# A diffusion block of pooling mixer, RG-LRU and ConvFFN: the sums of w_down, the second modulation rows and half of a modulation change their places

## The chip, the cores and the metric

The kernel runs on one core of a Trainium2 chip. The metric is device time in microseconds from launch to end. Engines are named as in the profile: PE is TensorE, DVE VectorE, ACT ScalarE, POOL GpSimd, SP SyncE. Each engine works through one queue in order; transfers are issued from SP's queue and from POOL's.

## The reference

One layer over 1024 latent tokens of width 1024 (a 16 x 64 grid) with 256 context tokens, float32.

```python
sh1, sc1, ga1, sh2, sc2, ga2 = split(silu(c) @ w_mod + b_mod, 6)
hx = rmsnorm(x, g_pre_mix) * (1 + sc1) + sh1            # hc likewise, from ctx and c_ctx
u_pool, u_lru, u_gate, g_pool, g_lru = split(h @ w_in)
y_pool = pooled windows of u_pool, less u_pool, @ pool_w, * pool_scale
y_lru  = (h_f + h_b) * gelu(u_gate)                     # two scans over conv(u_lru), context first
m = sigmoid(g_pool) * (y_pool @ w_proj_pool) + sigmoid(g_lru) * (y_lru @ w_proj_lru)
x = x + ga1 * rmsnorm(m @ w_out, g_post_mix)
g, u = split((rmsnorm(x, g_pre_ffn) * (1 + sc2) + sh2) @ w_up)
f = (gelu(conv3x3(g) + b) * u) @ w_down
x = x + ga2 * rmsnorm(f, g_post_ffn)
```

## The kernel before

All products run as three fp32r matmuls: each operand is split into a high and a low part (`split`: a cast on ScalarE, then a subtraction on VectorE), and hi*hi, hi*lo and lo*hi are summed. Weights come in tiles of 128 x 1024 (512 KB) through three SBUF buffers of the tag "raw" and are split into three buffers of the tag "whl" (`load_w`); so a load waits on SP's queue until a raw buffer is free, and a cast waits until a unit has left its whl buffer. Rows of w_mod, the short rows of `rowv`, x and w_up use the same three raw buffers.

The framework fixes the order of each engine's queue when the program is built, by the order of the program, moved by `high_priority` and `issue_after`; a tile is given out when an earlier one of its tag is released, which is after its last reader.

The stages, in order:
- **Start.** The first two parts of the modulation (`mod_block`), norm and transpose of x in two token halves, and `modulate`: high part on ScalarE, the product in float32 on GpSimd, low part on VectorE, for eight columns of 128 channels a half.
- **Input projections.** Units of 48 matmuls from hx for the pooled branch (`pool_unit`, `pool_out`), the u gates (`ug_unit`) and some g gates; results go to DRAM (yp_d, gl_d, sg_d) through GpSimd's queue. `mod_steps` walks over w_mod for the rows 0 and 1 of the later modulation (gate 1 and shift 2): eight loads of 512 KB, each multiplied into `acc` on VectorE; then `ones`-matmuls ("pm") add over the partitions, and one or two short rows, loaded into raw buffers, are added or multiplied to it, and the result is stored to row_d. `some(mods, 3)` makes three of the nine steps of a row.
- **LRU.** For each of eight channels of 128: `lru_in` (projection and convolution), `lru_scan` (gates, the square of r on GpSimd, two scans, times gl, store to yl_d), and a g gate. Rows 2 and 3 (scale 2, gate 2) of `mod_steps` go in between, three steps a channel.
- **Projections.** yp and yl are loaded by GpSimd's queue and split, six more g gates, then `pp_unit` (y_pool @ w_proj_pool) and `pl_unit` (y_lru @ w_proj_lru): pp 0 to 3, then pl 0, pp 4, pl 1, pp 5, pl 2, pp 6, pl 3, pp 7, pl 4 to 7. After pl 2, 3 and 4 `form_pair` loads two w_up tiles (ru, rg) and stores sums of them for the FFN. After pl 4 and 5 four tiles of w_out each are loaded. The results go to m_d.
- **Out projection**, x1, norm, second modulation and transposes for eight token tiles (L691 to L729).
- **FFN.** 24 blocks f of 128 channels; products in the form of Strassen and Winograd, seven half products of 12 matmuls a block (`mid`, `tail`, `head`), weights formed on VectorE (`weights`), a 3 x 3 convolution on VectorE (`post`), gu stored by GpSimd's queue. Beside it the queue sums quarters of w_down with accumulating DMAs in `n2raw` and stores them to sd_d (`sum_steps`): five steps for each of twelve p, three steps a block in the blocks 0 to 19.
- **Down projection**, again seven products, from w_down, sd_d and gu_d; `finish` normalises a token tile, adds x1 and stores it.

Of the kernel before, what the change touches and what calls it, by code (L numbers as in the profile page):

```python
# [14 lines left out]
D = 1024  # L15
# [25 lines left out]
def block_kernel(ctx: ExitStack, tc: tile.TileContext, x, cx, vecs, rowv, icnt, w_mod1, w_mod, w_in, pool_w,  # L41
# [58 lines left out]
    n2raw = gpool.tile([P, 4, 512], F32, name="n2raw", tag="n2raw")  # L100
    epsc = cpool.tile([P, 1], F32, name="epsc")
# [45 lines left out]
    def modulate(dst_hi, dst_lo, src, k, which):  # L147
        A.activation(dst_hi, src, AF.Identity, scale=S1[:, k, which:which + 1], bias=B1[:, k, which:which + 1])
        G.tensor_scalar(src, src, S1[:, k, which:which + 1], B1[:, k, which:which + 1],
                        op0=ALU.mult, op1=ALU.add)  # L150
        V.tensor_sub(dst_lo, src, f32(dst_hi))
# [10 lines left out]
    with tc.tile_pool(name="z0", bufs=1, reuse_waits="tile") as zp:  # L162
# [36 lines left out]
        def mod_x(h, k):  # L199
            modulate(hx[:, h, k, 0, :], hx[:, h, k, 1, :], xT[h][:, k, :], k, 0)  # L200
# [51 lines left out]
    def mod_steps(zp, pp, rng, nbuf):  # L252
# [4 lines left out]
        for j in rng:  # L257
            acc = zp.tile([P, D], F32, name=uid("acc"), tag="acc", bufs=1)
# [9 lines left out]
            ps = pp.tile([P, SEQ], F32, name=uid("pm"), tag="pu", bufs=nbuf)  # L268
# [18 lines left out]
    with tc.tile_pool(name="z1", bufs=1, reuse_waits="tile") as zp:  # L287
        n_unit = [0]
        mods = mod_steps(zp, pp, (0, 1), 3)
# [3 lines left out]
        def gate_unit(which, c):  # L293
# [5 lines left out]
            G.dma_start(sg_d[c, :, which, :], s)  # L299
# [57 lines left out]
        def ug_unit(c):  # L357
# [6 lines left out]
            G.dma_start(gl_d[c], gl)  # L364
            return mm

        def pool_out(g, o, after):
# [16 lines left out]
            G.dma_start(yp_d[c], yp)  # L384
# [69 lines left out]
    with tc.tile_pool(name="z2", bufs=1, reuse_waits="tile") as zp, \  # L454
# [3 lines left out]
        def gate_unit(which, c):  # L458
# [6 lines left out]
            G.dma_start(sg_d[c, :, which, :], s)  # L465
# [22 lines left out]
        def lru_scan(c, xp, xc, wg):  # L488
# [46 lines left out]
            G.dma_start(yl_d[c], y)  # L535

        gq = [(0, c) for c in range(6)] + [(1, c) for c in range(KT)]
        mods = mod_steps(zp, pp, (2, 3), 2)
        cur = lru_in(0)
        for c in range(KT):  # L540
            some(mods, 3)
# [12 lines left out]
    with tc.tile_pool(name="pj", bufs=1, reuse_waits="tile") as zp:  # L554
# [14 lines left out]
        for j, (which, c) in enumerate(gq):  # L569
# [5 lines left out]
            G.dma_start(sg_d[c, :, which, :], s)  # L575
# [20 lines left out]
        def pl_unit(c):  # L596
# [7 lines left out]
            G.dma_start(m_d[c], s)  # L604
# [4 lines left out]
        def piece():  # L609
            n_pc[0] += 1  # L610
            i = n_pc[0] % 5
# [24 lines left out]
        for c in range(4):  # L636
            pp_unit(c)
        for c in range(KT):
            m_last = pl_unit(c)
            if 2 <= c < 2 + NPF:  # L640
# [12 lines left out]

        h2 = H("h2")
# [98 lines left out]
    with tc.tile_pool(name="ff", bufs=1, reuse_waits="tile") as zp:  # L753
# [96 lines left out]
        def sum_steps(p):  # L850
            n2v = n2raw.rearrange("p (g h) c -> p g h c", g=2)
            lo, up = w_down[p * P:(p + 1) * P, :], w_down[(NH + p) * P:(NH + p + 1) * P, :]
            hv = lambda a: a.rearrange("p (h c) -> p h c", h=2)
            add = lambda dst, src: G.dma_start(dst, src, accum_op=ALU.add)  # L854
            yield G.dma_start(n2v[:, 0], hv(lo)), G.dma_start(n2v[:, 1], hv(up))
            yield (add(n2v[:, 1], hv(lo)), add(n2v[:, 0, 0, :], lo[:, 512:1024]),
# [302 lines left out]
```

## Time and profile before

| | us |
|---|---|
| times of three runs | 1632.53, 1640.2 (median), 1645.49 |
| the profiled execution, its time | 1641.79 |
| its span, from the first to the last instruction | 1640.0 |

The mean granted clock of TensorE is 0.987 of full speed in it. In the rows below, a line of a timeline gives start and length in us, engine and line, operation, what it writes and reads, how many such instructions it merges, and in brackets the idle time of that engine just before and who ended it. SPq is SP's queue issuing a DMA.

### The profile page before, as it was taken

How to read it: one execution, taken by the hardware profiler on the slowest of the kernel's cores; microseconds unless marked ns; L12 is line 12 of the kernel's file. 1: busy time of each engine (PE TensorE's matmuls, PEld its weight loads, DVE VectorE, ACT ScalarE, POOL GpSimd, SP SyncE). 2: the span in 40 equal slices, each digit the busy share in tenths (PEclk: the TensorE clock that was granted, in tenths of full speed). 3: DMA queues.
4: the chain of work that ended last, by engine and by line, in shares of the span. 5: the costliest groups of instructions: out<-in, count | busy, mean ns of one | idle time of the engine just before them, and what ended most of it. 6: DMA issues, size and time to landing. Idle time of an engine off the chain costs nothing.

```text
span 1640.0 us, 18320 instructions
## 1 busy us (share of the span) xinstructions
PE 1568.3 (96%) x6976; PEld 1265.2 (77%) x6976; DVE 1210.5 (74%) x1368; ACT 687.0 (42%) x828; POOL 239.3 (15%) x328
## 2 busy tenths in 40 slices
PE   6899999999999999999999989999899999999997
PEld 4588888877778788888788768877677777888885
DVE  7777664787887654354378889998798889787567
ACT  8523322565567734122143334333333334445442
POOL 1400200111112211010110122222222220000000
PEclk9999999999999999999999999999999999999999
DMA  8335454324233266399344567777667673687555
GB/s 314 114 103 165 138 184 139 127 97 148 84 103 116 90 232 230 124 289 300 131 141 142 209 195 186 193 199 197 176 183 180 178 187 110 217 320 256 175 188 192
DMA packets 98358, 289.15 MB, mean 176 GB/s; under 512 B 10871, under 2 KB 10999, under 8 KB 97502
## 3 DMA queue, kind: packets, MB, share of 16 engines
q1 hardware_dynamic: 60926, 170.64, 31.7%
q0 software_dynamic: 37344, 117.34, 24.2%
q8 instruction: 54, 0.88, 0.2%
q14 instruction: 34, 0.28, 0.1%
HBM read 221.34 MB, written 66.60 MB: 176 GB/s over the span
## 4 chain that ended last, share of the span: by engine, by line
PE 32%; DVE 10%; DMA 6%; ACT 2%; issue 2%; SPq 0%; DVEq 0%; ACTq 0%
PE pb L740 7%; PE pb L1017 6%; PE pb L706 5%; PE pc L740 4%; DMA raw<-in_w_up_dram 4%; PE pd L1017 4%; DVE gc L900 4%; PE pd L740 3%; PE pc L1017 2%; DVE wf L89 1%; DMA out_dram<-xr 1%; ACT wf L89 1%; DVE raw L801 0%; DMA xr<-x_d 0%; DVE w L89 0%
## 5 line engine op out<-in xcount | busy, mean ns | idle before, releaser
L242 PE MATMUL pu<-hx,whl 128*128 128x512 f32 x1056 | 266.7, 392 | 1.4 <-DVE whl L89 1.4
L900 DVE SCALAR_TENSOR_TENSOR gc<-gc,vec 128x945 f32<-128x945 f32 (+1 forms) x192 | 234.2, 1220 | 4.7 <-ACT gc L886 1.8
L89 ACT CAST whl<-raw 128x1024 fp32r<-128x1024 f32 (+1 forms) x109 | 109.1, 1003 | 305.8 <-DMA raw<-in_w_up_dram 74.4
L242 PEld LDWEIGHTS pu<-hx,whl 128*128 128x128 f32 x1056 | 186.8, 188 | 39.5 <-DVE whl L89 2.0
L89 DVE TENSOR_TENSOR whl<-raw,whl 128x1024 fp32r<-128x1024 f32 (+1 forms) x109 | 128.0, 1177 | 93.7 <-ACT whl L89 93.4
L242 PE MATMUL pg<-hx,whl 128*128 128x512 f32 x480 | 117.1, 396 | 0.0
L740 PE MATMUL pb<-h,wf 128*128 128x512 f32 x384 | 96.3, 400 | 11.3 <-ACT fk L810 11.3
L242 PEld LDWEIGHTS pg<-hx,whl 128*128 128x128 f32 x480 | 89.5, 191 | 19.3
L740 PEld LDWEIGHTS pb<-h,wf 128*128 128x128 f32 x384 | 71.8, 191 | 31.5 <-ACT fk L810 16.9
L740 PE MATMUL pb<-h,whl 128*128 128x512 f32 x384 | 94.9, 393 | 0.0
L706 PE MATMUL pb<-whl,mH 128*128 128x512 f32 x384 | 89.1, 392 | 1.0 <-ACT mH L700 1.0
L242 PE MATMUL pb<-hy,whl 128*128 128x512 f32 x384 | 87.8, 389 | 0.0
L706 PEld LDWEIGHTS pb<-whl,mH 128*128 128x128 f32 x384 | 71.5, 188 | 16.6 <-ACT mH L700 1.5
L740 PEld LDWEIGHTS pb<-h,whl 128*128 128x128 f32 x384 | 71.2, 188 | 16.9 <-ACT fk L810 2.5
L242 PEld LDWEIGHTS pb<-hy,whl 128*128 128x128 f32 x384 | 72.1, 188 | 14.9
L854 POOL DMA_DIRECT2D n2raw<-in_w_down_dram x72 | 63.0, 1006 | 122.9 <-DMA n2raw<-in_w_down_dram 122.6
L740 PE MATMUL pc<-nf,wf 128*128 128x512 f32 x288 | 72.9, 402 | 6.3 <-DVE gc L875 6.2
L1017 PE MATMUL pb<-hD 128*128 128x512 f32 x306 | 78.0, 390 | 0.0
L740 PEld LDWEIGHTS pc<-nf,wf 128*128 128x128 f32 x288 | 53.6, 190 | 22.5 <-DVE gc L875 11.5
L740 PE MATMUL pc<-nf,w 128*128 128x512 f32 x288 | 70.0, 391 | 0.2 <-DVE gc L847 0.2
L498 PE MATMUL pg<-xp,whl 128*128 128x512 f32 x192 | 61.3, 416 | 7.7 <-ACT i L504 7.6
L1017 PEld LDWEIGHTS pb<-hD 128*128 128x128 f32 x306 | 57.3, 188 | 12.3 <-DVE CA L1042 0.3
(319 smaller groups left out, 2986.9 us busy)
## 6 DMA issues: line engine op xcount, KB each, us to landing
raw<-in_w_up_dram SPq DMA_DIRECT2D x41, 512.0 KB, 4.6
raw<-in_w_in_dram SPq DMA_DIRECT2D x40, 512.0 KB, 4.7
n2raw<-in_w_down_dram POOLq DMA_DIRECT2D x36, 512.0 KB, 6.0
rawm<-in_w_mod_dram SPq DMA_DIRECT2D x32, 512.0 KB, 4.1
n2raw<-in_w_down_dram POOLq DMA_DIRECT2D x60, 256.0 KB, 5.7
rw<-gu_d SPq DMA_DIRECT2D x58, 256.0 KB, 5.1
gu_d<-gc POOLq DMA_DIRECT2D x24, 512.0 KB, 3.2
sd_d<-n2raw POOLq DMA_DIRECT2D x24, 512.0 KB, 4.6
```

Source lines behind the costliest of these rows:

```text
L89: return A.copy(hi, src), V.tensor_sub(lo, src, f32(hi))
L242: mm = T.matmul(ps[:, h * 512:(h + 1) * 512], wv[:, wi, k, :], act(h, k, ai), start=st, stop=sp)
L498: T.matmul(pg[:, h * 512:(h + 1) * 512], wg[:, wi, m, :], xp[:, ai, h * 512:(h + 1) * 512], start=(i == 0), stop=(i == 2))
L706: mm = T.matmul(ps[:, h * 512:(h + 1) * 512], mh[ai][:, k, :], wo[k][:, wi, h * 512:(h + 1) * 512], start=(k == 0 and i == 0), stop=(k == ...
L740: mm = T.matmul(ps, w(wi, j), b(ai, j), start=(start and j == 0 and i == 0), stop=(j == 3 and i == 2), skip_group_check=True)
L854: add = lambda dst, src: G.dma_start(dst, src, accum_op=ALU.add)
L900: V.scalar_tensor_tensor(o, gv[:, r0 + dr:r1 + dr, c0 + dc:c1 + dc], cw(i, j), o, op0=ALU.mult, op1=ALU.add)
L1017: T.matmul(bank[dst](t), op[:, gi, 512 + t * P:512 + (t + 1) * P], op[:, wi, H0], start=(first and p == 0 and i == 0), stop=(p == NH - 1 a ...
```

## The change

Four things are moved or altered.
- `sum_steps` is defined ahead of all stages, and `sum_step` issues one step behind a given DMA of GpSimd's queue: behind every store of sg, gl, yp, yl and m until 45 steps are made (18 in the input projections, 16 in the LRU, 11 up to the store of m of pl 4); the other 15 follow one a block from f = 2 of the FFN.
- Rows 2 and 3 of `mod_steps` leave the LRU loop and are made after pl_unit 0 to 5, three steps each. `acc` takes the buffer bc2 and pm the bank c; the ring of pieces in `form_pair` has four buffers for five.
- In the second token half the modulation product of even columns is made by VectorE.
- x1 of the token tiles 0 to 3, which are finished last, is loaded into the first half of N behind the matmuls of product 5.

```diff
@@ beside n2raw, ahead of all stages @@
+    def sum_steps(p):
+        n2v = n2raw.rearrange("p (g h) c -> p g h c", g=2)
+        lo, up = w_down[p * P:(p + 1) * P, :], w_down[(NH + p) * P:(NH + p + 1) * P, :]
+        hv = lambda a: a.rearrange("p (h c) -> p h c", h=2)
+        add = lambda dst, src: G.dma_start(dst, src, accum_op=ALU.add)
+        yield G.dma_start(n2v[:, 0], hv(lo)), G.dma_start(n2v[:, 1], hv(up))
+        yield (add(n2v[:, 1], hv(lo)), add(n2v[:, 0, 0, :], lo[:, 512:1024]),
+               add(n2v[:, 0, 1, :], lo[:, 0:512]))
+        yield add(n2v[:, 1, 0, :], lo[:, 512:1024]), add(n2v[:, 0, 0, :], up[:, 512:1024])
+        yield add(n2v[:, 1, 0, :], up[:, 512:1024]),
+        yield tuple(G.dma_start(sd_d[p, i], n2v[:, i].rearrange("p h c -> p (h c)")) for i in range(2))
+
+    dsteps = [st_ for p in range(NH) for st_ in [sum_steps(p)] * 5]
+    n_step = [0]
+
+    def sum_step(after, limit=45):
+        if n_step[0] >= limit:
+            return after
+        with tc.issue_after(after.ins):
+            i = next(dsteps[n_step[0]])[-1]
+        n_step[0] += 1
+        return i
...
-    def modulate(dst_hi, dst_lo, src, k, which):
+    def modulate(dst_hi, dst_lo, src, k, which, eng=G):
         A.activation(dst_hi, src, AF.Identity, scale=S1[:, k, which:which + 1], bias=B1[:, k, which:which + 1])
-        G.tensor_scalar(src, src, S1[:, k, which:which + 1], B1[:, k, which:which + 1],
+        eng.tensor_scalar(src, src, S1[:, k, which:which + 1], B1[:, k, which:which + 1],
                         op0=ALU.mult, op1=ALU.add)
...
-            modulate(hx[:, h, k, 0, :], hx[:, h, k, 1, :], xT[h][:, k, :], k, 0)
+            modulate(hx[:, h, k, 0, :], hx[:, h, k, 1, :], xT[h][:, k, :], k, 0, V if h and k % 2 == 0 else G)
...
-    def mod_steps(zp, pp, rng, nbuf):
+    def mod_steps(new_acc, new_ps, rng):
...
-            acc = zp.tile([P, D], F32, name=uid("acc"), tag="acc", bufs=1)
+            acc = new_acc()
...
-            ps = pp.tile([P, SEQ], F32, name=uid("pm"), tag="pu", bufs=nbuf)
+            ps = new_ps()
@@ the same edit at the stores of sg (three places), gl, yp, yl and m @@
-            G.dma_start(sg_d[c, :, which, :], s)
+            sum_step(G.dma_start(sg_d[c, :, which, :], s))
@@ LRU stage @@
-        mods = mod_steps(zp, pp, (2, 3), 2)
         cur = lru_in(0)
         for c in range(KT):
-            some(mods, 3)
             nxt = lru_in(c + 1) if c + 1 < KT else None
@@ projections @@
-            i = n_pc[0] % 5
+            i = n_pc[0] % 4
...
             pp_unit(c)
+        mods = mod_steps(lambda: zp.tile([P, D], F32, name=uid("acc"), tag="bc2"), lambda: pbank("c"), (2, 3))
         for c in range(KT):
             m_last = pl_unit(c)
+            some(mods, 3)
             if 2 <= c < 2 + NPF:
                 form_pair(c - 2)
@@ FFN @@
-            for _ in range(3):
-                g = next(steps, None)
-                if g is not None:
-                    with tc.issue_after(chain[-1].ins):
-                        chain.append(next(g)[-1])
+            if f > 1:
+                chain.append(sum_step(chain[-1], 60))
@@ down projection @@
+        def load_x(xr, tt):
+            nc.sync.dma_start(xr, x1_d[tt * P:(tt + 1) * P, :].rearrange("p (h c) -> p h c", h=2))
+
         def finish(h, t):
             tt = 4 * h + t
-            xr = zp.tile([P, 2, 512], F32, name=uid("xr"), tag="xr", bufs=2)
-            nc.sync.dma_start(xr, x1_d[tt * P:(tt + 1) * P, :].rearrange("p (h c) -> p h c", h=2))
+            xr = N[:, 0, 2 * t:2 * t + 2, :] if h == 0 else zp.tile([P, 2, 512], F32, name=uid("xr"), tag="xr", bufs=2)
+            if h:
+                load_x(xr, tt)
...
+            if q == 5:
+                for t in range(4):
+                    load_x(N[:, 0, 2 * t:2 * t + 2, :], t)
```


## Rows read from the trace of the kernel before

**Rows 1.** Page, parts 1 and 2: busy us (share) xcount; PE busy tenths in 40 slices.

```profile
PE 1568.3 (96%) x6976; PEld 1265.2 (77%) x6976; DVE 1210.5 (74%) x1368; ACT 687.0 (42%) x828; POOL 239.3 (15%) x328
...
PE   6899999999999999999999989999899999999997
```

**Rows 2.** Windows: PE, PEld, DVE, ACT, POOL busy (xcount), clock, DMA share, GB/s.

```profile
720.00:760.00 40.00, 40.00 (x179) 33.13 (x178) 20.02 (x22) 10.30 (x12) 4.33 (x7) 1.00 0.97 323
```

**Rows 3.** Timeline of POOL in the LRU: y stores (L535), square (L514).

```profile
343.74 0.54 POOL L535 DMA_DIRECT2D yl_d<-i  x1 [15.59 <-DVE i L534]
349.22 2.55 POOL L514 TENSOR_TENSOR a<-r 128x1280 f32<-128x1280 f32 x1 [4.94 <-ACT r L512]
...
491.22 0.56 POOL L535 DMA_DIRECT2D yl_d<-i  x1 [13.16 <-DVE i L534]
...
523.97 0.54 POOL L535 DMA_DIRECT2D yl_d<-i  x1 [14.78 <-DVE i L534]
```

**Rows 4.** Timeline of all engines in the LRU: start, us, engine, line.

```profile
358.59 1.88 PE L270 MATMUL pm<-acc,ones 128*128 128x512 f32 x4
...
362.40 1.21 DVE L273 TENSOR_TENSOR acc<-pm,rowb 1x1024 f32<-1x1024 f32 x1
...
375.50 0.73 DVE L264 TENSOR_SCALAR acc<-rawm,cs 128x1024 f32<-128x1024 f32 x1
...
385.90 1.04 ACT L89 CAST whl<-raw 128x1024 fp32r<-128x1024 f32 x1 [4.22 <-DMA raw<-in_w_in_dram]
...
388.02 1.22 PE L498 MATMUL pg<-xp,whl 128*128 128x512 f32 x2 [3.79 <-ACT i L504]
```

**Rows 5.** Timeline of SP's queue in the LRU.

```profile
328.57 2.84 SPq L255 DMA_DIRECT2D rowb<-in_rowv_dram  x2
...
354.86 0.35 SPq L94 DMA_DIRECT2D raw<-in_w_in_dram  x1
```

**Rows 6.** Timeline of SP's queue in the projections.

```profile
681.86 0.33 SPq L619 DMA_DIRECT2D raw<-in_w_up_dram  x1
...
748.45 0.33 SPq L94 DMA_DIRECT2D raw<-in_w_out_dram  x1
...
769.75 5.20 SPq L709 DMA_DIRECT2D xr<-in_x_dram  x3
```

**Rows 7.** Timeline of all engines in the projections.

```profile
685.37 0.62 ACT L89 CAST pc<-raw 128x512 fp32r<-128x512 f32 x1 [4.84 <-DMA raw<-in_w_up_dram]
...
711.91 11.04 PE L242 MATMUL pb<-hy,whl 128*128 128x512 f32 x48
```

**Rows 8.** Timeline of POOL in the FFN: stores of gu, blocks 2, 8, 20.

```profile
991.11 0.54 POOL L917 DMA_DIRECT2D gu_d<-gc  x1 [12.74 <-DVE gc L913]
...
1107.00 0.56 POOL L917 DMA_DIRECT2D gu_d<-gc  x1 [4.40 <-DVE gc L913]
...
1363.56 0.53 POOL L917 DMA_DIRECT2D gu_d<-gc  x1 [5.10 <-DVE gc L913]
```

**Rows 9.** Timeline of all engines in the FFN.

```profile
1164.84 1.04 ACT L89 CAST whl<-raw 128x1024 fp32r<-128x1024 f32 x1 [11.09 <-DMA raw<-in_w_up_dram]
...
1167.37 5.23 PE L740 MATMUL pd<-h,wf 128*128 128x512 f32 x12 [5.20 <-ACT fk L810]
```

**Rows 10.** Line 681, the FFN's w_up loads, 960 to 1400 us.

```profile
DMA to landing us min/median/max: 3.8/5.1/8.5
```

**Rows 11.** Timeline of the end, all engines.

```profile
1629.96 1.28 DVE L1049 SCALAR_TENSOR_TENSOR xr<-CA,rs,xr 128x1024 f32<-128x1024 f32 x1 [2.34 <-DMA xr<-x_d]
...
1635.55 1.42 DVE L1049 SCALAR_TENSOR_TENSOR xr<-CA,rs,xr 128x512 f32<-128x512 f32 x2 [0.94 <-DMA xr<-x_d]
```

**Rows 12.** Timeline of POOL in the start: modulation products.

```profile
58.87 0.77 POOL L149 TENSOR_SCALAR xT<-xT,S,B 128x512 f32<-128x512 f32 x1 [7.65 <-ACT hx L148]
61.67 9.74 POOL L149 TENSOR_SCALAR xT<-xT,S,B 128x512 f32<-128x512 f32 x8 [2.03 <-ACT hx L148]
```

**Rows 13.** Page, part 5: busy us, mean ns of one, idle before.

```profile
L854 POOL DMA_DIRECT2D n2raw<-in_w_down_dram x72 | 63.0, 1006 | 122.9 <-DMA n2raw<-in_w_down_dram 122.6
```

More of the change, by code (lines that the diff above doesn't have):

```diff
@@ L288, in block_kernel @@
         n_unit = [0]
-        mods = mod_steps(zp, pp, (0, 1), 3)
+        mods = mod_steps(lambda: zp.tile([P, D], F32, name=uid("acc"), tag="acc", bufs=1),
+                         lambda: pp.tile([P, SEQ], F32, name=uid("pm"), tag="pu", bufs=3), (0, 1))
         wload = lambda u: wq.pop(0)
@@ L363, in ug_unit @@
             A.activation(gl, pu, AF.Gelu_apprx_tanh)
-            G.dma_start(gl_d[c], gl)
+            sum_step(G.dma_start(gl_d[c], gl))
             return mm
@@ L383, in pool_out @@
                         V.tensor_scalar(yp[:, hs], ps, vcol("pool_scale", c), None, op0=ALU.mult)
-            G.dma_start(yp_d[c], yp)
+            sum_step(G.dma_start(yp_d[c], yp))
         ctx_t = {}
@@ L464, in gate_unit @@
                 A.activation(s, ps, AF.Tanh, scale=0.5)
-            G.dma_start(sg_d[c, :, which, :], s)
+            sum_step(G.dma_start(sg_d[c, :, which, :], s))
         LC = SEQ
@@ L534, in lru_scan @@
             V.tensor_mul(y, y, gl)
-            G.dma_start(yl_d[c], y)
+            sum_step(G.dma_start(yl_d[c], y))
         gq = [(0, c) for c in range(6)] + [(1, c) for c in range(KT)]
-        mods = mod_steps(zp, pp, (2, 3), 2)
         cur = lru_in(0)
         for c in range(KT):
-            some(mods, 3)
             nxt = lru_in(c + 1) if c + 1 < KT else None
@@ L574, in block_kernel @@
             A.activation(s, ps, AF.Tanh, scale=0.5)
-            G.dma_start(sg_d[c, :, which, :], s)
+            sum_step(G.dma_start(sg_d[c, :, which, :], s))
         hy = H("hy")
@@ L603, in pl_unit @@
             V.tensor_add(s, s, mp)
-            G.dma_start(m_d[c], s)
+            sum_step(G.dma_start(m_d[c], s))
             return s
@@ L652, in block_kernel @@
         ga1g, B2, S2 = bcs
+        assert n_step[0] == 45
         h2 = H("h2")
@@ L848, in mid @@
             st[f] = (gc, u2)
[L850 to L856, printed above, removed]
-                   add(n2v[:, 0, 1, :], lo[:, 0:512]))
-            yield add(n2v[:, 1, 0, :], lo[:, 512:1024]), add(n2v[:, 0, 0, :], up[:, 512:1024])
-            yield add(n2v[:, 1, 0, :], up[:, 512:1024]),
-            yield tuple(G.dma_start(sd_d[p, i], n2v[:, i].rearrange("p h c -> p (h c)")) for i in range(2))
-        steps = iter([st_ for p in range(NH) for st_ in [sum_steps(p)] * 5])
         chain = []
```

## Prediction

> **What bounds the kernel.** I read the page's engine list first: TensorE is busy for 1568.3 us, 96% of the span [rows 1], and the change leaves its instructions what they are. So only about 72 us of idle time, and what the clock loses after it, are to be had, and I asked stage by stage which wait makes them. Four stages matter.
>
> The LRU stage: the stores of y, one for each channel, run from 343.74 to 523.97 us [rows 3], 180.2 us for five channels; the last of these, after the modulation rows were done, took 32.75 us. Five of them would be 163.8 us, so 16.5 us are lost. The stalls are of one kind: ScalarE waits 4.22 us at the head of its queue for a w_in load, the tanh behind it comes late, and TensorE waits 3.79 us [rows 4]. The load is late because the three buffers of the tag "raw" hold w_mod rows.
>
> The projections: TensorE has no gap, though DMA is busy for 97% of the stretch shown [rows 2]. Their slack is in the prefetch through "raw", and it is used below.
>
> The FFN: the stores of gu show its pace. Blocks 2 to 8 take (1107.00 - 991.11) / 6 = 19.3 us each, the next twelve (1363.56 - 1107.00) / 12 = 21.4 us [rows 8]; the difference over twelve blocks is 24.8 us. There ScalarE, at 1164.84, casts a w_up load for which it waited 11.09 us; the fork copy behind that cast makes TensorE wait 5.20 us, and its next 12 matmuls take 5.23 us [rows 9] where 48 take 11.04, that is 2.76 for 12 [rows 7]. After that idle TensorE ran at the lower of its two levels, 1.2 instead of 2.4 GHz, and such an idle costs some 2.5 us more in clock. Such loads land after 3.8 to 8.5 us, median 5.1 [rows 10], beside the accumulating DMAs of the w_down sums.
>
> The end: the last two additions of x1 wait 2.34 and 0.94 us for their loads [rows 11].
>
> **The change, part by part.**
>
> *Modulation on VectorE.* In the second token half GpSimd's eight products take 9.74 us in a row, 1.22 each, and one that ran alone took 0.77 [rows 12]. VectorE's tensor_scalar of twice the width takes 0.73 us [rows 4], so 0.37 to 0.73 for this one. VectorE also subtracts for every column, so its queue gets longer as GpSimd's gets shorter: the gain lies between 0 and half of the 9.74. Whatever it is would be kept, since TensorE is full in every slice that follows, up to the LRU stage [rows 1]. I take 1 us, near the low end, since 1.22 beside 0.77 says that the two engines already get in each other's way.
> The Trainium skill (SBUF — State Buffer, "Who interferes with whom") has a rule against this part: VectorE and GpSimd lock a shared port pair for a whole instruction, and VectorE takes it in its two-port modes, which tensor_scalar can enter. The 0.77 and 1.22 us agree with a lock for two-input operations; no run here shows it yet for tensor_scalar. By it the gain would be the low end, 0.
>
> *The w_down sums.* 45 of 60 steps leave the FFN; 15 stay, one a block instead of three. Each accumulating issue costs GpSimd 1.0 us [rows 13], at most three a step. Ahead of the FFN they stand behind stores of sg, gl, yp, yl and m on GpSimd's queue, and behind them wait memsets, the LRU's squares, the loads of yp and yl and the stores of the formed weights. Between an LRU channel's y store and the next square lie 5.5 us (343.74 to 349.22 [rows 3]), which cover three issues; a step's predecessor was issued a store earlier and has landed, except where stores come close together, as those of the six gates ahead of the projections do. I cost all this at 0. If the cover goes, a blocked step costs what the predecessor's landing still takes, about 5 us at the median of [rows 10], and the loads of yl behind it have more slack than that, since the first unit that needs them comes after all those gates and four other units.
> In the FFN the w_up loads then meet a third of the other traffic in blocks 2 to 16 and none after. If they land in about 3.8 instead of 5.1 us, two on the chain of each two blocks, the pace of 19.3 us is there again: 24.8 us at best. Nothing at worst, if VectorE sets the late pace. I take 23, and 2 for the first blocks, in whose window the sums now start: 25.
>
> *The second modulation rows leave the LRU.* 16 loads, 16 VectorE passes and 4 short row loads go, and two sets of ones-matmuls (1.88 us each [rows 4]) move with them. The stage gains the 16.5 us above; at least the 3.8 us of matmuls, at most 20, my estimate with a fifth of 16.5 for one channel more. I take 16.5.
>
> *They come under the last projections.* This is the dear part. The four row loads use the "raw" buffers too, and a row is let go only by the addition behind the ones-matmuls. In the LRU two rows were loaded from 328.57 us, their first use was at 362.40, right behind the matmuls of 358.59, and from 331.4 to 354.86 no "raw" load was issued [rows 4, 5]. The LRU lived on one buffer. Now the ones-matmuls stand on TensorE's queue behind pl_unit(2), while SyncE's queue next holds form_pair(0), which needs two buffers at once, and behind it the weights of the very next unit, pp_unit(6).
> First stall: pl_unit(2) ends at 711.91 + 10.9 = 722.8 [rows 7]. The matmuls end at 724.7, the first row is let go at 726, and only then can rg be issued (before: 681.86 [rows 6]), with pp_unit(6)'s weights after it at about 727.5. A load lands 3.5 us after issue at best (rg: 681.86 to its cast at 685.37 [rows 6, 7]), a cast takes 1 us: TensorE goes on at 733 to 734.5 instead of 724.7. 9 us.
> Second: between that rg and the weights of pl_unit(5) lie 18 loads (pp, pl, 3 w_mod, ru, rg, pp, pl, 3 w_mod, ru, rg, 4 w_out), so 19 intervals. At its fastest the ring issued nine loads in a row, the first at 748.45 and the last at 769.75 [rows 6], 2.7 us apart; 3.2 is my estimate where formed pairs hold two buffers for longer. Issue falls at 777 to 788, use 5 to 6 us later; TensorE wants it at 734 + 4 x 10.9 = 778. 4 to 15, I take 10.
> Third: the two row loads of the last set again hold two buffers until after pl_unit(5), and four w_out loads pass through the third before pl_unit(6)'s weights: the first stall again, with two loads more to issue, 12 us.
> With 2.5 us of clock for each, 31 + 7 = 38, and 3.8 of matmuls that the LRU no longer has: 42 us lost. Bounds: 12, if the rows don't clog the ring (matmuls and a slower ring), and 55 if landings grow to 6.5 us in a stage where DMA is 97% busy.
> The formed pieces have four buffers for five, so each pair waits once for a store; that is within the pace of 3.2 us.
>
> *x1 for the last tokens* is loaded at product 5 into N's first half, done with since product 3. 2.34 + 0.94 us go, less what an earlier stop hides: 3 (0 to 4).
>
> **Sum.** On the profiled execution, 1641.8 us (span 1640.0): -1 - 16.5 + 42 - 25 - 3 = -3.5, so 1638. The median of the runs shown is 1.6 us below that execution: 1637 us.
>
> **Rivals.**
> *The ring isn't clogged*: the rows are loaded or let go earlier, because the order of SyncE's queue or TensorE's puts pm ahead of waiting units. Then the projections lose 12 and the sum is -33: 1606. Against it: in the LRU the matmuls stood behind every earlier unit, and the rows were held 33 us [rows 4, 5].
> *Slower, from the FFN*: its late pace isn't made by landings but by VectorE and the order on ScalarE's queue; once a cast is behind, the loop of release, load, cast and release keeps its 21.4 us. It decides if ScalarE still stands 5 us and more at such a cast with the loads landing in 4. Then 25 becomes 5 and the clog stays: 1657. For it: the first blocks kept 19.3 us with three steps a block beside them [rows 8]. Against it: landings up to 8.5 us where the stalls are [rows 9, 10].
> *Worse projections*: the bound of 55 holds with all else as forecast: 1650, more if GpSimd's waits delay the loads of yl.
>
> **How the numbers follow.** Forecast 45%, 1637 within some 11 us; ring not clogged 25%, 1606; FFN not mended 20%, 1657; worse projections 10%, 1650 to 1665. The range takes in the second case and the third, with some 3 us beside them: 1602 to 1660. Outside it lie the upper half of the fourth, and a ring without clog with the other terms at their best. What a measurement of this kernel can tell from no change is about 1%, 16 us (its three runs lie 13 us apart): all but a little of the second case is faster by that, most of the third and half of the fourth is slower at or beyond it. Faster 0.31, same 0.46, slower 0.23.
>
> **What would show it.** Right: in the LRU all y stores some 33 us apart and no cast waiting 4 us for w_in; in the projections two row loads long before pm, rg issued right behind the row addition, idle TensorE before pp_unit(6), pl_unit(5) and pl_unit(6), and the last projection ending 35 to 45 us later than its start in the LRU's gain would give; FFN blocks near 19.3 us to the end with w_up landing in about 4; no wait on x1 at the end. Wrong: no gap in the projections, FFN blocks that slow to 21 us again, or new waits of the LRU's squares behind a sum step. What would upset the forecast most is another order of the "raw" loads than the program's.

## The result, and the profile of the changed kernel

The changed kernel takes 1682.0 us (median of four runs, 1680.85 to 1683.37), the kernel before 1642.9 (four runs beside it): a ratio of 1.025 (95% interval 1.020 to 1.030). It is slower by some 39 us, where 1637 was forecast and the range ended at 1660. The profiled execution's span is 1681.1 us, 41.1 more than the 1640.0 of before.

The page first, its parts 1 and 2, to hold against [rows 1]:

```profile
PE 1570.1 (93%) x6976; PEld 1268.6 (75%) x6976; DVE 1225.6 (73%) x1372; ACT 683.2 (41%) x828; POOL 236.3 (14%) x324
...
PE   6999999999998988969399998999999999999997
PEclk9999999999999998989699999999999999999999
```

TensorE has the same 6976 matmuls. Its slices dip at the 15th to 20th (about 590 to 840 us), with the granted clock, and hardly elsewhere: the loss sits there. To size it I take from TensorE's timeline the start of the first matmul of each stage, here and in four of the kernels below (us, one trace each; "first stage" is the input projections, "FFN, down" goes to the end of the span):

| | first stage | LRU | six gates | pp 0 to 3 | pl 0 to pl 7 | out proj. | FFN, down |
|---|---|---|---|---|---|---|---|
| before | 249.1 | 279.5 | 65.5 | 43.5 | 131.8 | 92.8 | 747.0 |
| changed | 252.5 | 270.3 | 73.0 | 53.7 | 186.3 | 92.9 | 721.1 |
| small_only | 247.0 | 280.0 | 65.4 | 43.5 | 131.5 | 92.9 | 736.9 |
| sums_back | 246.3 | 261.0 | 65.4 | 43.5 | 182.4 | 92.8 | 739.8 |
| mods_back | 251.6 | 309.7 | 68.3 | 52.2 | 132.3 | 92.9 | 721.8 |
| after_placed | 247.6 | 261.2 | 67.0 | 43.5 | 191.5 | 92.8 | 722.4 |

From before to changed: +3.4 - 9.2 + 7.5 + 10.2 + 54.5 + 0.1 - 25.9, and 0.6 at the start, make 41.2.

GpSimd's timeline in the LRU, against [rows 3]:

```profile
348.49 0.53 POOL L559 DMA_DIRECT2D yl_d<-i  x1 [14.22 <-DVE i L558]
349.02 0.93 POOL L105 DMA_DIRECT2D n2raw<-in_w_down_dram  x1
355.12 0.55 POOL L111 DMA_DIRECT2D sd_d<-n2raw  x1 [5.17 <-DMA n2raw<-in_w_down_dram]
355.68 2.34 POOL L538 TENSOR_TENSOR a<-r 128x1280 f32<-128x1280 f32 x1
...
423.63 0.86 POOL L105 DMA_DIRECT2D n2raw<-in_w_down_dram  x1 [5.78 <-DMA n2raw<-in_w_down_dram]
424.20 2.65 POOL L538 TENSOR_TENSOR a<-r 128x1280 f32<-128x1280 f32 x1
```

Behind the y store stand two steps in a row, not one: the step meant for the gate's store is queued there too. The second waits until the first has landed, and the square stands behind it; in [rows 3] GpSimd had been free for it 4.94 us ahead.

The cover of 5.5 us between y store and square, on which the forecast counted, was itself made by the stalls of the old LRU. sums_back, below, has the modulation rows out of the LRU and no steps in it, and there the square follows the y store after 1.8 us:

```profile
342.67 0.54 POOL L559 DMA_DIRECT2D yl_d<-i  x1 [16.80 <-DVE i L558]
344.45 2.32 POOL L538 TENSOR_TENSOR a<-r 128x1280 f32<-128x1280 f32 x1 [1.24 <-ACT r L536]
```

So one part of the change took away the cover that another part needed. With the steps the square comes 7.2 us behind the y store (348.49 to 355.68), 5.4 late.

The same in the projections. GpSimd's timeline, then ScalarE's and TensorE's:

```profile
583.86 1.84 POOL L105 DMA_DIRECT2D n2raw<-in_w_down_dram  x2
584.98 1.28 POOL L588 DMA_DIRECT2D st<-yp_d  x1
593.94 0.86 POOL L105 DMA_DIRECT2D n2raw<-in_w_down_dram  x1 [7.68 <-DMA n2raw<-in_w_down_dram]
594.50 1.41 POOL L588 DMA_DIRECT2D st<-yp_d  x2
...
647.99 0.53 POOL L111 DMA_DIRECT2D sd_d<-n2raw  x1 [6.35 <-DMA n2raw<-in_w_down_dram]
648.52 1.06 POOL L601 DMA_DIRECT2D st<-yl_d  x2
```

```profile
598.86 1.05 ACT L89 CAST yps<-st 128x1024 fp32r<-128x1024 f32 x1 [16.12 <-DMA st<-yp_d]
...
653.62 1.05 ACT L89 CAST hy<-st 128x1024 fp32r<-128x1024 f32 x1 [7.32 <-DMA st<-yl_d]
```

```profile
614.78 12.57 PE L265 MATMUL pb<-hx,whl 128*128 128x512 f32 x48 [5.91 <-ACT whl L89]
...
667.71 13.35 PE L265 MATMUL pd<-yps,whl 128*128 128x512 f32 x48 [7.68 <-DVE sgp L615]
```

Loads of yp and yl are issued behind steps that wait; ScalarE stands at their casts with the weights' casts behind, and TensorE waits 5.91 and 7.68 us, the second time for VectorE's pass over pd (L615), which is queued behind subtractions of yl. The 48 matmuls behind such a wait take 12.57 and 13.35 us where 48 take 11.04 [rows 7]: behind the idle time the granted clock is 0.53 from 614.8 to 618.0 us and 0.50 from 667.7 to 671.0, that is the lower of TensorE's two levels, 1.2 GHz, and 1.00 from 618 and from 674 us on.

Now the forecast's own stalls. SP's queue, against [rows 6], and TensorE:

```profile
696.32 2.50 SPq L278 DMA_DIRECT2D rowb<-in_rowv_dram  x2
...
739.13 0.33 SPq L641 DMA_DIRECT2D raw<-in_w_up_dram  x1
740.38 0.33 SPq L94 DMA_DIRECT2D raw<-in_w_pp_dram  x1
```

```profile
735.30 1.02 PE L293 MATMUL pc<-acc,ones 128*128 128x512 f32 x2
...
750.05 13.19 PE L265 MATMUL pc<-yps,whl 128*128 128x512 f32 x48 [12.87 <-ACT whl L89]
...
812.99 12.47 PE L265 MATMUL pb<-hy,whl 128*128 128x512 f32 x48 [17.10 <-ACT whl L89]
...
842.07 14.15 PE L265 MATMUL pb<-hy,whl 128*128 128x512 f32 x52 [14.89 <-ACT whl L89]
```

Rows at 696, ones-matmuls at 735, only then rg and the weights of pp_unit(6): the three stalls stand where they were forecast. But the row is not all that holds rg back. SP's waits from 690 to 745 us (total, times, longest):

```profile
SPq L607 <- DVE sgp L625: 25.6, 3, 15.7
...
SPq L641 <- DVE acc L296: 0.7, 1, 0.7
```

Ahead of rg (L641) the queue stands 15.7 us at a load of a gate into sgp (L607), whose buffer VectorE's last pass for pl_unit(2) frees at 738.0 us. It then waits only 0.7 us for the row's addition (L296), which ends at 739.1. Both end behind pl_unit(2), and the forecast had the second alone.

The stretch of [rows 2] now reads, by windows:

```profile
720.00:760.00 40.00, 27.13 (x108) 21.29 (x107) 14.15 (x16) 5.00 (x7) 6.20 (x9) 0.83 0.70 197
```

In the FFN GpSimd's stores of gu for blocks 2, 8 and 20, against [rows 8], and the landing of the w_up loads (L706 now), against [rows 10]:

```profile
1054.07 0.54 POOL L929 DMA_DIRECT2D gu_d<-gc  x1 [21.60 <-DVE gc L925]
...
1171.55 0.54 POOL L929 DMA_DIRECT2D gu_d<-gc  x1 [15.68 <-DVE gc L925]
...
1407.77 0.53 POOL L929 DMA_DIRECT2D gu_d<-gc  x1 [17.08 <-DVE gc L925]
```

```profile
DMA to landing us min/median/max: 3.3/3.6/4.2
```

Blocks 2 to 8 take 19.6 us each, 8 to 20 19.7 instead of 21.4. At the end the additions of the last four tiles no longer wait for x1. In the start, GpSimd and VectorE, against [rows 12]:

```profile
63.04 1.15 POOL L172 TENSOR_SCALAR xT<-xT,S,B 128x512 f32<-128x512 f32 x1 [2.74 <-ACT hx L171]
64.45 5.06 POOL L172 TENSOR_SCALAR xT<-xT,S,B 128x512 f32<-128x512 f32 x3 [0.26 <-ACT hx L171]
```

```profile
64.83 0.54 DVE L172 TENSOR_SCALAR xT<-xT,S,B 128x512 f32<-128x512 f32 x1
...
66.92 0.92 DVE L172 TENSOR_SCALAR xT<-xT,S,B 128x512 f32<-128x512 f32 x1
```

### The profile page after: what moved, and what is told of

Same layout as the page of the kernel before. It is cut to its first block, busy times and chain, and to the rows that moved or that the text cites. A ratio compares the mean times of both kernels' runs of the same rounds, so it can differ in the third digit from the quotient of the medians.

```text
span 1681.1 us, 18317 instructions
## 1 busy us (share of the span) xinstructions
PE 1570.1 (93%) x6976; PEld 1268.6 (75%) x6976; DVE 1225.6 (73%) x1372; ACT 683.2 (41%) x828; POOL 236.3 (14%) x324
## 5 line engine op out<-in xcount | busy, mean ns | idle before, releaser
L89 DVE TENSOR_TENSOR whl<-raw,whl 128x1024 fp32r<-128x1024 f32 (+1 forms) x109 | 138.4, 1272 | 64.4 <-ACT whl L89 64.1
L265 PE MATMUL pb<-hy,whl 128*128 128x512 f32 x384 | 91.8, 400 | 32.0 <-ACT whl L89 32.0
L929 POOL DMA_DIRECT2D gu_d<-gc x24 | 13.1, 548 | 431.3 <-DVE gc L925 431.3
L289 DVE SCALAR_TENSOR_TENSOR acc<-rawm,cs,acc 128x1024 f32<-128x1024 f32 x28 | 35.9, 1284 | 45.8 <-DMA rawm<-in_w_mod_dram 45.8
```

The costliest lines, as they stand in the source:

```text
L89: return A.copy(hi, src), V.tensor_sub(lo, src, f32(hi))
L265: mm = T.matmul(ps[:, h * 512:(h + 1) * 512], wv[:, wi, k, :], act(h, k, ai), start=st, stop=sp)
L289: V.scalar_tensor_tensor(acc, raw, cs[:, k, 0:1], acc, op0=ALU.mult, op1=ALU.add)
L929: chain.append(G.dma_start(gu_d[f], gc[:, 1, :]))
```

## The experiments

Theory after the result: the sum steps, costed at 0, block GpSimd's queue and cost some 15 to 18 us under the gates and the first pp units; the rows that hold raw buffers make the rest of the loss in the projections. Rivals: the bytes, of the sums and of the w_mod blocks, rather than waits and buffers. Ratios are to the kernel before, with 95% intervals.

**One part undone at a time.** *mods_back*: the second modulation back in the LRU. *sums_back*: all 60 steps back in the FFN, three a block. *small_only*: both back. mods_back and small_only have five buffers for the pieces again.

```diff
 # mods_back, again in the LRU's loop and not behind pl_unit
+            some(mods, 3)
 # sums_back
-        if n_step[0] >= limit:
+        if limit == 45 or n_step[0] >= limit:
...
-            if f > 1:
-                chain.append(sum_step(chain[-1], 60))
+            for _ in range(3):
+                if n_step[0] < 60:
+                    chain.append(sum_step(chain[-1], 60))
```

> The changed kernel with the second modulation back in the LRU loop, all else as changed. Theory (the rows make the loss in the projections, the sum steps on GpSimd's queue only some 15 us of it, and the FFN's 22 us come from the sums): projections 255 us instead of 313, LRU some 8 us longer, FFN at 19.7 us a block: about 1633 (1625 to 1642). Rival (the sum steps on GpSimd's queue are what slows the projections, by holding back the loads of yp and yl): projections still above 285 us, time 1655 or more.

> The changed kernel with all 60 steps of the w_down sums back in the FFN, three a block, all else as changed. Theory: the FFN goes back to 21.4 us a block (+22), the stalls ahead of pl_unit(0) go (-18), the three stalls by the rows stay: 1675 to 1690. Rival (the sum steps are what slows the projections): 1645 to 1660. If the FFN keeps 19.7 us a block although the sums are back in it, its gain came from somewhere else.

> The kernel before with only the two small parts: VectorE takes half of the modulation products of the second token half, and x1 for the last tokens is loaded at product 5. Theory: 1 us at the start and 3 at the end, so 4 us less than before (0 to 6). Rival (VectorE and GpSimd get in each other's way, or the products now wait in VectorE's queue): nothing gained at the start, 0 to 3 us from the end alone.

Measured: mods_back 1659.1 us (1.011, 1.008 to 1.014), sums_back 1662.2 (1.014, 1.011 to 1.017), small_only 1634.3 (0.996, 0.994 to 0.998). Over small_only the spread sums alone cost 25 us, the moved modulation alone 28. mods_back is a miss: the projections are good again, as the theory had it (253 us from the first gate on), but the LRU takes 39 us more than in the changed kernel, where 8 were expected; beside the w_mod blocks the steps hurt there more than without. sums_back lies between its two expectations, 2 us above the rival's: the rows' three stalls stay (40 us), but the steps' part is twice the 18 us I had counted. small_only gains 8 us instead of 4. In its trace 2.1 us of that are in the first stage and 10.1 in the FFN and down projection, where x1 is worth 2.9 (10.98 us from the last matmul's end to the last instruction, now 8.03); the other 7 come in a stage that the edit does not touch.

**Queue or bytes of the sums.** *thin_sums* is mods_back with an eighth of the columns a step; *sums_placed* is mods_back with all columns, the steps put elsewhere.

```diff
 # thin_sums, every step of the first nine pairs
-    def sum_steps(p):
+    def sum_steps(p, w=64):
...
-        hv = lambda a: a.rearrange("p (h c) -> p h c", h=2)
+        hv = lambda a: a.rearrange("p (h c) -> p h c", h=2)[:, :, 0:w]
 # sums_placed, two of its edits; gates of the LRU and of the projections lose their steps as the y store does
-                G.tensor_mul(a2, r, r)
+                sq = G.tensor_mul(a2, r, r)
+                if d:
+                    sum_step(sum_step(sq))
...
-            sum_step(G.dma_start(yl_d[c], y))
+            G.dma_start(yl_d[c], y)
```

> The kernel with the second modulation back in the LRU (mods_back, 1659), where each step of the w_down sums ahead of the FFN moves an eighth of its columns: the same issues in the same places, waiting for each other in the same way, with an eighth of the bytes. What is left out: seven eighths of the sums of the first nine pairs; the down product reads w_down rows in their place, of the same size. mods_back takes 814 us from the first projection unit to the out projection, the kernel with the small parts alone 767: 47 us lost. Theory (GpSimd's queue stands at a step until the step before it has landed, and what is queued behind comes late): at least 30 of the 47 us stay, time 1643 to 1660. Rival (the bytes of the sums fill the DMA engines and delay the weights): under 12 of the 47 us stay, time below 1628.

> mods_back with its sum steps put where GpSimd has nothing to do: in the LRU two steps behind the second square of each channel instead of one behind the y store and one behind the gate's store; none behind the two pooled outputs ahead of the context rows, none behind the six gates and the y store at the start of the projections; 40 steps ahead of the FFN, 20 in it. Nearly the same bytes in nearly the same stretch. Theory (the queue): of the 47 us lost ahead of the out projection less than 20 stay and the FFN keeps its gain of 15: about 1630 (1622 to 1640). Rival (the bytes): 35 us and more stay, 1647 or above.

In sums_placed the last pair's sums are partly overwritten, since its steps reach the blocks that copy u into n2raw; its instructions are the same. Measured: thin_sums 1630.2 (0.993, 0.990 to 0.995), 13.5 of the 47 us left, between the two expectations; sums_placed 1629.3 (0.992, 0.990 to 0.995), 11.7 left. The landing times tell why thin steps help although they stand in the same places. DMA issues in the LRU, mods_back and then thin_sums (count, KB, median us to landing):

```profile
raw<-in_w_in_dram SPq DMA_DIRECT2D x20, 512.0 KB, 3.9
...
n2raw<-in_w_down_dram POOLq DMA_DIRECT2D x15, 256.0 KB, 5.8
```

```profile
raw<-in_w_in_dram SPq DMA_DIRECT2D x20, 512.0 KB, 4.2
...
n2raw<-in_w_down_dram POOLq DMA_DIRECT2D x15, 32.0 KB, 4.7
```

The weights land no later beside full steps, so the bytes don't delay them. With the modulation back in the LRU GpSimd has 5.4 us from the first y store to the square (small_only). An issue and the landing of a thin step, 4.7 us, nearly fit: the square comes after 6.1 us. A full one lands after 5.8 to 7.8 us, and the square comes after 7.0 (mods_back). Under the gates and the first pp units, where steps stand in a row, thin ones still cost 7.9 us where full ones cost 11.6 (116.8 and 120.5 against 108.9 in small_only). By the waits, VectorE stands 23.8 us at squares in the LRU of small_only, 37.0 in mods_back, 26.6 in thin_sums and 23.4 in sums_placed. GpSimd's timeline of sums_placed shows a wait where nobody waits for it:

```profile
355.57 2.74 POOL L540 TENSOR_TENSOR a<-r 128x1280 f32<-128x1280 f32 x1 [4.83 <-ACT r L538]
...
362.82 0.54 POOL L111 DMA_DIRECT2D sd_d<-n2raw  x1 [2.58 <-DMA n2raw<-in_w_down_dram]
...
376.16 0.56 POOL L563 DMA_DIRECT2D yl_d<-i  x1 [12.03 <-DVE i L562]
```

The same placing in the changed kernel itself is *after_placed*: 40 steps ahead of the FFN instead of 45, and the steps in the FFN end by block 18.

> The changed kernel with nothing but its sum steps put elsewhere: in the LRU both behind the second square, none behind the two pooled outputs ahead of the context rows nor at the start of the projections, 40 ahead of the FFN and 20 in it. Theory (steps that stand in front of a square, of the loads of yp and yl or of a store that frees a buffer cost the changed kernel some 30 us: 6 in the first stage, 9 in the LRU, 8 under the gates, 10 under the first pp units): these go, 1682 becomes 1648 to 1662; what stays above 1634 is the second modulation. Rival (the stalls by the raw buffers come later and swallow what is gained earlier): 1670 or more.

1659.4 (1.013, 1.010 to 1.016): 22.6 us less than the changed kernel. Ahead of pl_unit(0) 30.2 us come back (table), and 5.2 are lost again behind it. So the steps' place is what cost them; for the changed kernel this is shown. Under the gates the bytes move away with the steps, and there it is thin_sums that speaks against the bytes.

**The rows.** *rows_early* takes the rows in ahead of the ones-matmuls; *rows_acc_free* also frees acc early; *mods_thin* thins the w_mod blocks in it.

```diff
 # rows_early
+            if j > 1:
+                r0 = row(j)
+                fac = gpool.tile([P, D], F32, name=uid("facb"), tag="raw", bufs=3)
+                nc.sync.dma_start(fac, rowv[j + 3:j + 4, :].to_broadcast([P, D]))
+                with tc.high_priority(offset=MPRI):
+                    V.scalar_tensor_tensor(acc[0:1, :], r0, 3.0 - j, acc[0:1, :], op0=ALU.add, op1=ALU.add)
+                    V.tensor_mul(acc, acc, fac)
             ps = new_ps()
 # mods_thin
+                w = P if j > 1 and k else D
-                nc.sync.dma_start(raw, w_mod[k * P:(k + 1) * P, j * D:(j + 1) * D])
+                nc.sync.dma_start(raw[:, 0:w], w_mod[k * P:(k + 1) * P, j * D:j * D + w])
```

> The changed kernel, with the four short rows of the second modulation taken in before the ones-matmuls (the bias row added to partition 0 of acc, acc multiplied by the factor row broadcast to all partitions), so that no row holds a raw buffer until TensorE has done a matmul. As many loads as before, two of them wider. Theory (the held buffers make the stalls): the idle time of 12.9, 17.1 and 14.9 us ahead of pp_unit(6), pl_unit(5) and pl_unit(6) falls to under 10 us in all, the projections go from 313 to some 270 us, the time from 1682 to about 1638 (1630 to 1648). Rival (the 16 w_mod loads as such are too much for a ring and DMA engines that are full): the stalls move to other units and keep 30 us or more, time 1665 to 1685.

> The changed kernel with rows taken in early (rows_early, 1670.6) and in addition the finished modulation row copied out of PSUM into two half rows of their own, so that acc is free as soon as the ones-matmuls have read it. In rows_early VectorE stands 7.6 us at the first product of the last set, at 749, until the row is stored from acc, and three w_mod blocks hold all raw buffers meanwhile. Theory (that wait makes part of the stall of 18 us ahead of pl_unit(5)): it falls to 10 us or less, the time to 1656 to 1664. Rival (the ring or the DMA engines can't bring 18 blocks in that time anyway): the stalls stay, 1667 or more.

> rows_acc_free (1665.4: the changed kernel, rows taken in early, acc freed early), where 14 of the 16 w_mod blocks under the projections bring and add only 128 of their 1024 columns. What is left out: seven eighths of these products of the second modulation. As many loads in the same order through the same buffers. From pl_unit(0) to the out projection rows_acc_free takes 171 us, the kernel with the small parts alone 131.5. Theory (what is left of the loss are the bytes: DMA is busy for 0.99 of the time from 757 to 800 us, at 400 GB/s): under 145 us, time 1632 to 1642. Rival (the order of SyncE's queue, which stands at loads of sgp and raw whose buffers TensorE's units free): 158 us or more, time 1652 or above.

Measured: rows_early 1670.6 (1.019, 1.016 to 1.023), from pl_unit(0) to the out projection 175.2 us instead of 186.3; rows_acc_free 1665.4 (1.014, 1.012 to 1.017), 171.2; mods_thin 1658.9 (1.012, 1.009 to 1.015), 163.7. All three miss their theory: 11 us, then 4, then 7.5 in that stretch, one trace each; the intervals of the whole times overlap from each kernel to the next. The bytes are a small part here too: seven eighths of them are worth at most these 7.5 us. VectorE's timeline of rows_early shows what took the place of the rows:

```profile
740.64 1.20 DVE L304 COPY acc<-pc 1x1024 f32<-1x1024 f32 x1
749.49 0.75 DVE L287 TENSOR_SCALAR acc<-rawm,cs 128x1024 f32<-128x1024 f32 x1 [7.64 <-issue]
```

The next set's first product needs acc, which has one buffer, until the finished row has been stored from it (issued at 742.81 us, landed 6.6 us later); its w_mod blocks sit in all raw buffers until then. In mods_thin, with acc freed by the ones-matmuls themselves, that product still runs only at 737.33 us, behind them (733.53).

**Both holders apart.** In sums_back n2raw is idle at this time, so it can hold two acc. All four kernels here have that; *two_acc_sums* is two_acc with 30 steps of the sums at the places of sums_placed.

```diff
 # two_acc (rows early); two_acc_4pc: four piece buffers; two_acc_rows: rows as in the change
+        accs = [n2raw[:, o:o + 2, :].rearrange("p a b -> p (a b)") for o in (0, 2)]
-        mods = mod_steps(lambda: zp.tile([P, D], F32, name=uid("acc"), tag="bc2"), lambda: pbank("c"), (2, 3))
+        mods = mod_steps(lambda: accs.pop(0), lambda: pbank("c"), (2, 3))
```

> The second modulation under the projections with the sums back in the FFN (sums_back: 1662, 182 us from pl_unit(0) to the out projection), rows taken in ahead of the ones-matmuls, and each of the two sets with an acc of its own, in n2raw, which the sums don't use at that time; so no raw buffer waits for TensorE, and the pieces have their fifth buffer again. As many blocks and bytes. Theory (buffers held until TensorE is done are the loss): 133 to 145 us, time 1615 to 1627. Rival (20 more loads are too many for three raw buffers and the in-order queue): 160 us or more, 1640 or above.

> two_acc with four buffers for the five pieces of a formed pair, as in the changed kernel. Theory (the fifth piece waits once for a store, within the slack): at most 4 us more than two_acc. Rival (a piece that waits for its store keeps two raw buffers, and that is what is left of the loss): 8 us or more above two_acc.

> two_acc with the rows as in the changed kernel, used only behind the ones-matmuls. Theory (each held row pair makes a stall by itself): TensorE idle for 8 to 15 us ahead of pp_unit(6) and again ahead of pl_unit(6), 20 to 30 us more than two_acc. Rival (the single acc was what mattered): within 6 us of two_acc.

> two_acc with 30 steps of the sums in the first stage and the LRU, where GpSimd has nothing to do, and 30 in the FFN, three in two blocks instead of six. Theory: the FFN gains 8 to 15 us at 2 to 5 us lost ahead of it: 5 to 12 us below two_acc, 1606 to 1618. Rival (the FFN keeps its pace of 20.4 us a block unless a block has one step): the same as two_acc or above.

Measured: two_acc 1642.4 (1.001, 0.999 to 1.003), two_acc_4pc 1637.9 (1.000, 0.997 to 1.002), two_acc_rows 1667.0 (1.017, 1.013 to 1.021), two_acc_sums 1628.1 (0.994, 0.991 to 0.996), 14 below two_acc, more than the 5 to 12 expected. From pl_unit(0) to the out projection: 159.8, 152.6, 182.0 and 159.6 us. A second acc alone is worth nothing (182.0 against 182.4 in sums_back); with the rows early as well 22 to 29 us go. With the rows early rg also stands in front of those loads of sgp in SP's queue (in rows_early it is issued at 705.09 us), so these 22 to 29 us are the price of using the rows late, by the buffers that they hold and by the order that the build then gives the queue; no run takes the two apart. The fifth piece buffer is worth nothing that shows. two_acc misses its theory by 15 us and comes out at its rival's 160 us and 1640; TensorE and VectorE in two_acc_4pc show one more holder:

```profile
715.59 13.56 PE L265 MATMUL pc<-yps,whl 128*128 128x512 f32 x48 [9.08 <-DVE n2raw L304]
```

```profile
714.33 1.21 DVE L304 COPY n2raw<-pc 1x1024 f32<-1x1024 f32 x1
```

pp_unit(6) uses PSUM bank c, into which the ones-matmuls wrote, and VectorE copies the row out only behind a formed pair. *bank_d* moves them to bank d (`pbank("d")`) in two_acc_sums with four piece buffers; *bank_d_g* is bank_d with all modulation products on GpSimd.

> two_acc_sums with four piece buffers and the ones-matmuls of the second modulation in PSUM bank d, which no unit needs for two units, instead of c, which the next one needs. Theory (that bank makes 9 of the 21 to 28 us that are still lost under the projections): no idle time ahead of pp_unit(6), 140 to 147 us from pl_unit(0) to the out projection, time 1608 to 1620. Rival (the unit behind it is late by then for its weights): 150 us or more, 1622 or above.

> bank_d with all modulation products on GpSimd, as in the kernel before. Theory: the last hx column comes 2 to 3 us later, at 72 instead of 69, and nothing behind it takes that back: 1 to 4 us above bank_d. Rival (VectorE and GpSimd hold each other up, as the rule on the shared port has it): the same time within 1 us, or less.

bank_d takes 1622.5 us (0.989, 0.986 to 0.991), the fastest of all; bank_d_g 1629.5 (0.993, 0.991 to 0.995). In bank_d nothing waits ahead of pp_unit(6), yet this stretch still takes 153.6 us: TensorE now stands at pl_unit(5).

```profile
758.87 13.19 PE L265 MATMUL pb<-hy,whl 128*128 128x512 f32 x48 [10.56 <-ACT whl L89]
```

So the rival had this part right. SP's queue ahead of it, and its longest wait from 720 to 760 us:

```profile
738.14 1.53 SPq L94 DMA_DIRECT2D raw<-in_w_out_dram  x2
747.48 0.33 SPq L685 DMA_DIRECT2D bc<-row_d  x1
...
750.32 0.56 SPq L94 DMA_DIRECT2D raw<-in_w_pl_dram  x1
```

```profile
SPq L685 <- DMA wf_d<-pc: 7.7, 1, 7.7
```

The queue stands 7.7 us at the load of a finished row into a buffer that it shares with the formed pieces, until a piece has been stored; a w_out tile and the weights of pl_unit(5) are queued behind. That is one more holder by the trace, and no run removes it.

The products on VectorE are worth 7 us, more than the 1 to 4 expected; 3.7 of them show in the first stage (247.2 against 250.9 us), where GpSimd's eight products again take 9.74 us in bank_d_g.

**Other places for the second modulation.** *mods_z1* and *best1* put it into the first stage (more `m` steps in the list of units), *placed_rows_lru* leaves it in the LRU with rows early.

> The kernel with the small parts alone, the sums in the FFN, and the second modulation neither in the LRU nor under the projections but in the first stage of projections from x, where DMA is busy for 0.40 to 0.45 of the time; twelve groups of three steps there instead of six, all rows taken in ahead of the ones-matmuls. Theory (the place makes the loss, not the 16 blocks as such): the LRU takes 261 us as without the second modulation, the first stage at most 8 us more, 1634 becomes 1614 to 1628. Rival (16 more blocks through three raw buffers stall any stage): the first stage loses 18 us or more, 1634 or above.

> All 32 w_mod blocks in the first stage of projections from x, two steps behind each unit, the ones-matmuls one step later than the last product and rows taken in ahead of them; sum steps where GpSimd has nothing to do, x1 early, half the products on VectorE. mods_z1 lost 21 us in two stalls of the first stage, 13.8 of them where TensorE stood at the ones-matmuls for acc. Theory (TensorE no longer meets a product that isn't done): first stage 247 to 253 us, LRU 262 to 265, FFN with the gain of 15: 1600 to 1614. Rival (three raw buffers don't bring that many blocks beside the units' weights): first stage 262 us or more, 1620 or above.

> The second modulation in the LRU as in the kernel before, its rows taken in ahead of the ones-matmuls, the sum steps where GpSimd has nothing to do (the steps left in the FFN are over by block 18), x1 early and half the modulation products on VectorE. Theory (in the LRU too the two rows that hold raw buffers for some 30 us make the late w_in casts): the LRU takes 270 to 276 us instead of 284, time 1614 to 1622. Rival (the 16 blocks themselves make the casts late): LRU 281 or more, time 1626 or above.

mods_z1 1642.1 (1.000, 0.998 to 1.002): the LRU 261.2 us as expected, the first stage 275.4. best1 1628.7 (0.994, 0.992 to 0.995): the first stage 269.7. The rival is right in both: three buffers and VectorE's queue don't bring that many blocks in time. Both stand at the ones-matmuls, here in best1's TensorE timeline:

```profile
120.78 3.75 PE L303 MATMUL pm<-acc,ones 128*128 128x512 f32 x4 [14.36 <-DVE acc L299]
```

placed_rows_lru 1646.8 (1.005, 1.003 to 1.006) is a plain miss: the LRU takes 299.5 us, not 270 to 276. By its waits SP's queue stands 14.0 us at a w_mod block for a product that waits for acc, and ScalarE 67.6 us at w_in casts against 53.4 in sums_placed. My reading is that with the rows out of the way the next w_mod blocks fill the buffers; no run tests it.

## Why the prediction was wrong

The step that failed is **"I cost all this at 0"** for the 45 sum steps on GpSimd's queue. Changed less sums_back, they cost 6.2 us in the first stage, 9.3 in the LRU, 7.6 under the gates, 10.2 under the first pp units and 3.9 behind: 37 us of the 44.6 by which the sum was off. Moving the steps alone gave back 30.2 of the 33.3 us ahead of pl_unit(0) (after_placed). Each reason for the 0 failed by itself. "A step's predecessor was issued a store earlier" holds for the program, not for the queue, where two steps stand in a row. The 5.5 us of cover were read in an LRU with modulation rows; without them 1.8 us are left, and even 5.5 do not hold an issue and a landing of 5.8 to 7.8 us. The yp loads had no slack at all. The yl loads had some up to the unit that reads them, but their casts and subtractions stand ahead of the pp units' weights and passes in ScalarE's and VectorE's queues, and these came late. The price of one blocked step, about 5 us, was near (waits of 5.17, 5.78 and 7.68 us), though by luck, since [rows 10] are SP's loads and not these additions; it was written down and then left out of the sum and of the range. The sign that it named for being wrong, squares that wait behind a sum step, is what came. The Trainium skill (DMA: Bandwidth & Descriptors, Anatomy of one DMA — SWDGE (gpsimd) path) says that a DMA's semaphore wait happens on the issuing sequencer before dispatch; the trace agrees, with the square of 355.68 us behind a wait of 5.17.

The other terms:
- *Projections, +42.* Right in place and 9 us too small: 50.9 us (182.4 in sums_back against 131.5), with stalls of 10.9, 15.5 and 13.7 for 9, 10 and 12 (12.9, 17.1 and 14.9 in the changed kernel). In mechanism it was half of it: rows used late are 22 to 29 us (two_acc and two_acc_4pc against two_acc_rows), by their buffers or by the loads of sgp that stand ahead of rg. The forecast saw the rows alone; behind them acc and bank c hold the same units, and removing one gave little each time. The ones-matmuls' 3.8 us apart, some 18 us stay in bank_d; the shared buffer of the finished row is part of them by the trace, and how the rest divides between the pace of three raw buffers and SP's queue standing at loads of sgp was not told apart.
- *LRU, -16.5.* Right: -18.5 in sums_back. The steps took 9.3 of it back.
- *FFN, -25.* Right in mechanism, somewhat too large: the stage and the down projection are 25.9 us shorter together, 3 of them x1; landings 3.6 us, blocks of 19.7. Against sums_back, which has the sums in the FFN and x1 early, it is 18.7, and against small_only 15.8, so part of the 25.9 is the spread of the stage from run to run. That 23 came out beside 25 is in part luck.
- *x1, -3.* Right: -2.9 in small_only.
- *Modulation, -1.* Too small: 2.1 to 3.7 us in the first stage (small_only against before, bank_d against bank_d_g). The low end was chosen since the engines hold each other up. They do (GpSimd's three products take 1.69 us each in the mean beside VectorE's, instead of 1.22; VectorE's take 0.54 and 0.92 beside GpSimd's), and half the products still pay. By the Trainium skill (SBUF — State Buffer, Who interferes with whom) a VectorE instruction in a two-port mode and a GpSimd instruction block each other for the whole instruction. The forecast took a gain of 0 from that, which does not follow: even one behind the other, four of 1.22 and four of 0.54 us are 7.0 instead of 9.74, an estimate from the rows shown. Nor does the trace show a whole block, with VectorE's 0.54 us at 64.83 inside a GpSimd product.

The rival "worse projections" named the missing piece, waits of GpSimd that delay loads, at 10% and on yl alone.

## What to carry to other kernels

A DMA that must wait for the one before it is a blocking instruction: look up in the built order of the queue, not in the program, what stands between the two, and price each at issue plus landing less that distance, with the distance that the other parts of the change leave; put it where the engine's next work is further away than that, here behind the last square of a channel (22.6 us for moving nothing but steps). In a shared ring list for every buffer which engine's instruction frees it; where that is one at the end of a longer queue, expect a stall, and expect a second holder behind the first. Work moved out of a stage with idle time into one without has to fit its buffers, not only its busy shares.

## What the runs showed of the hardware

In the LRU, from issue to landing in the median: GpSimd's accumulating DMAs of 32 KB take 4.7 us (thin_sums) and of 256 KB 5.8 (mods_back), so most of the time is not bytes. It is not the adding alone either: of the nine of 512 KB in mods_back (7.8 us), six are plain copies on the same queue, and these take 7.4, where SP's plain loads of 512 KB of w_in take 3.9 beside them. Those loads are not slowed: 3.8 us before, 3.9 in mods_back.
